# Sums of weights one piece later, and the second pass in the order P3, P7, P6, in a TensorE-bound decoder trunk

## The chip, the core and the metric

The kernel runs on one core of a Trainium2 chip. The metric is the device time of one execution in microseconds; the times before are three runs of the same program, and one further execution was profiled.

## What is computed

Two residual layers on 256 tokens of width 2048: the first has differential attention as its mixer, the second a Mamba-2 mixer, and each mixer is followed by a dense MLP of width 8192. The change lies in the MLPs:

```python
def sq_relu_mlp(h, w1, w2):
    return jnp.square(jax.nn.relu(h @ w1)) @ w2

for i in range(DEPTH):
    hn = rms_norm(h, mixer_norm[i])
    ...
    h = h + mix.astype(h.dtype)
    h = h + sq_relu_mlp(rms_norm(h, mlp_norm[i]), mlp_w1[i], mlp_w2[i]).astype(h.dtype)
```

All inputs are float32. The kernel keeps that accuracy by splitting every operand into a rounded high part and a low rest and by multiplying high by high, high by low and low by high.

## The kernel before

**Weights.** A unit of weights is 128 x 1024 floats (512 KB). `load` (L181) takes one of five `raw` buffers and issues the transfer on SP's queue (L186). `split_weights` (L153) takes one of four `w` buffers: ScalarE casts the raw weights into the high half (L158), and VectorE subtracts that from the raw weights to give the low half (L159). TensorE needs the cast for the first four matmuls of a product and the subtraction for the last two.

**The first matrix of an MLP** is cut into eight column blocks. One is done plainly (`blocks`, kind "s"), seven by a scheme of Strassen's kind (`seven`, L547, kind "S"): a 2 x 2 division of the product with seven products P1 to P7 in place of eight. `product` (L552) issues six 512-column matmuls (L557, L559) for one piece of one product: four with the high half of the weights, two with the low half. The activations' sums (S1 to S4) are made once for an MLP by `sum_parts` (tile `sa`); P1, P2 and P4 use plain activations (tile `act`). The weights' sums are made by VectorE for every unit: L569 (b11 - b12, kept in tile `wsum`), L579 (b22 - b12, in place of b12), L584 (adds b22 to `wsum`), L600 (subtracts b21 from `wsum`). Each of the four lines runs 4 times in a block, 7 blocks in each of two MLPs, 56 times in all.

`seven` is a generator in three passes of four steps. A step of the first pass issues a piece of P1 and one of P5; of the second, P7, P3 and P6; of the third, P2 and P4. Behind every piece it pauses (`yield`).

**What comes in the pauses.** `mlp` (L610) drives the blocks of the next quarter against the second matrix of this one: for each piece of W2 (`token_steps`, L224: a load, a cast, a split and 12 matmuls at L238 and L240) it lets the generator go on by some 58/30 = 1.9 pieces (L699 to L709). In the pauses there are also bits of side work (`side.tick`): the expansion of finished blocks into activations (L640: transposes at L656, cast L263, subtraction L264) and, at the end of a W2 block, the update of the residual (L716). In the first block of an MLP the partner is the plainly done column block (`wide_steps`, L169 and L173).

**PSUM.** P1, P5, P7, P6, P2 and P4 and the transposes share three `aux` slots; P3 has the slot `aux1` alone in the MLP. A slot comes free when VectorE or ScalarE has read it (L264, L574, L575, L587 to L591, L603, L604).

**Order.** The queue of each engine is ordered by the framework in which the kernel is written. It takes the order of the text as a preference and may put forward an instruction whose inputs are ready earlier; on the chip each queue then runs in that fixed order, and the waits between the engines are put in by the framework too.

Of the kernel before, what the change touches and what calls it, by code (L numbers as in the profile page):

```python
# [16 lines left out]
ALU = mybir.AluOpType  # L17
# [74 lines left out]
def trunk_kernel(ctx: ExitStack, tc: tile.TileContext, x, xt, par, rope, qk, wv, wo, w10, w10s, w20, win, wdt, wout, w11, w11s, w21, out):  # L92
    nc = tc.nc
    V, S, G, PE = nc.vector, nc.scalar, nc.gpsimd, nc.tensor
# [23 lines left out]
    def aux():  # L118
        return ps.tile([P, 512], F32, tag="aux", bufs=3, name="aux")

    def aux1():
        return ps.tile([P, 512], F32, tag="aux1", bufs=1, name="aux1")
# [30 lines left out]
    def split_weights(raw, n=1):  # L153
        w = wp.tile([P, 2, 1024], F32R, tag="w", bufs=4, name="w")
        wh, wl = w[:, 0, :], w[:, 1, :]
        for i in range(n):
            s = slice(1024 // n * i, 1024 // n * (i + 1))
            S.copy(out=wh[:, s], in_=raw[:, s])  # L158
            V.tensor_tensor(out=wl[:, s], in0=raw[:, s], in1=wh[:, s].bitcast(F32), op=ALU.subtract)  # L159
        return wh, wl  # L160
# [20 lines left out]
    def load(src, n=1):  # L181

        raw = wp.tile([P, 1024], F32, tag="raw", bufs=5, name="raw")
        w = 1024 // n
        for i in range(n):
            nc.sync.dma_start(out=raw[:, i * w:(i + 1) * w], in_=src[:, i * w:(i + 1) * w])  # L186
        return raw
# [137 lines left out]
    with tc.tile_pool(name="xin", bufs=1) as xp:  # L325
# [13 lines left out]
        for g in range(4):  # L339
# [4 lines left out]
            for b in range(4):  # L344
                c = slice(512 * (g % 2), 512 * (g % 2 + 1))
                src = raw[g // 2][b][:, c]
# [200 lines left out]
    def seven(pool, src, sas, u):  # L547


        a = [None] * 4  # L550

        def product(pp, which, w, i):  # L552
            for j, wj in enumerate(w):
                for kp in range(2):
                    ah, al = sas[2 * i + kp][which]
                    m = wj[:, kp * NB:(kp + 1) * NB]
                    PE.matmul(pp, lhsT=ah, rhs=m, start=(i + kp + j == 0), stop=(i == 3 and kp + j == 2))  # L557
                    if j == 0:
                        PE.matmul(pp, lhsT=al, rhs=m, start=False, stop=False)  # L559

        A11, S4, A12, S1, S3, S2, A22 = range(7)
        p1, p5 = aux(), aux()
        for i in range(4):
            while len(sas) < 2 * i + 2:
                side.tick()
            b11, b12 = load(src[0, i]), load(src[1, i])
            a[i] = pool.tile([P, 1024], F32, tag="wsum", bufs=4, name="wsum")
            w = split_weights(b11)
            V.tensor_tensor(out=a[i], in0=b11, in1=b12, op=ALU.subtract)  # L569
            product(p1, A11, w, i)  # L570
            yield
            product(p5, S1, split_weights(a[i]), i)
            yield
        S.copy(out=u[:, 0, 0], in_=p1)  # L574
        S.copy(out=u[:, 1, 1], in_=p5)  # L575
        p7, p3, p6 = aux(), aux1(), aux()
        for i in range(4):
            b12, b22 = load(src[1, i]), load(src[2, i])
            V.tensor_tensor(out=b12, in0=b22, in1=b12, op=ALU.subtract)  # L579
            product(p7, S3, split_weights(b12), i)  # L580
            yield
            product(p3, S4, split_weights(b22), i)
            yield
            V.tensor_tensor(out=a[i], in0=b22, in1=a[i], op=ALU.add)  # L584
            product(p6, S2, split_weights(a[i]), i)
            yield
        V.tensor_tensor(out=u[:, 0, 1], in0=p6, in1=u[:, 0, 0], op=ALU.add)  # L587
        V.tensor_tensor(out=u[:, 1, 0], in0=p7, in1=u[:, 0, 1], op=ALU.add)
        V.tensor_tensor(out=u[:, 0, 1], in0=u[:, 0, 1], in1=u[:, 1, 1], op=ALU.subtract)
        V.tensor_tensor(out=u[:, 0, 1], in0=p3, in1=u[:, 0, 1], op=ALU.add)  # L590
        V.tensor_tensor(out=u[:, 1, 1], in0=u[:, 1, 0], in1=u[:, 1, 1], op=ALU.subtract)  # L591
        for t in range(2):
            S.activation(u[:, t, 1], u[:, t, 1], AF.Relu)
            S.activation(u[:, t, 1], u[:, t, 1], AF.Square)
        p2, p4 = aux(), aux()
        for i in range(4):
            b21 = load(src[3, i])
            product(p2, A12, split_weights(b21), i)
            yield
            V.tensor_tensor(out=a[i], in0=a[i], in1=b21, op=ALU.subtract)  # L600
            product(p4, A22, split_weights(a[i]), i)
            yield
        V.tensor_tensor(out=u[:, 0, 0], in0=p2, in1=u[:, 0, 0], op=ALU.add)  # L603
        V.tensor_tensor(out=u[:, 1, 0], in0=u[:, 1, 0], in1=p4, op=ALU.subtract)  # L604
        for t in range(2):
            S.activation(u[:, t, 0], u[:, t, 0], AF.Relu)
            S.activation(u[:, t, 0], u[:, t, 0], AF.Square)
        yield

    def mlp(xs, w1, w1s, w2, pool, after):  # L610
# [21 lines left out]
        def hidden(c):  # L632
            us[c] = u = pool.tile([P, 2, 2, NB], F32, tag="u", bufs=2, name="u")
            n = kinds[:c].count(kinds[c])
            if kinds[c] == "s":
                yield from blocks(n, u)
            else:
                yield from seven(pool, w1s[n], sas, u)
# [438 lines left out]
```

## Time and profile before

| what | value |
|---|---|
| median of 3 runs | 2449.77 us (2448.08 to 2452.68) |
| the profiled execution | 2449.62 us, span of its instructions 2447.9 us |
| TensorE matmuls, busy | 2434.1 us, 12050 instructions |
| VectorE, busy | 2098.2 us, 2591 instructions |
| ScalarE, busy | 1535.6 us, 2154 instructions |
| moved by DMA | 500.54 MB, mean 204 GB/s |
| a weight load, issue to landing | 4.3 to 4.4 us in the median for the MLPs' weights |

In the rows PE is TensorE's matmul side and PEld its weight loads, DVE is VectorE, ACT ScalarE, SP the queue that issues the loads. A row of a group gives the line, the engine, the operation, the tile written and those read, the shapes, the count, the busy time with the mean of one in ns, and the idle time just before with what ended it. The span of a matmul is modelled and overlaps the next one, so starts are to be compared rather than ends. The MLPs lie at about 395 to 1070 us and 1740 us to the end; the blocks done by seven products end at about 978 and 2336 us.

### The profile page before, as it was taken

How to read it: one execution, taken by the hardware profiler on the slowest of the kernel's cores; microseconds unless marked ns; L12 is line 12 of the kernel's file. 1: busy time of each engine (PE TensorE's matmuls, PEld its weight loads, DVE VectorE, ACT ScalarE, POOL GpSimd, SP SyncE). 2: the span in 40 equal slices, each digit the busy share in tenths (PEclk: the TensorE clock that was granted, in tenths of full speed). 3: DMA queues.
4: the chain of work that ended last, by engine and by line, in shares of the span. 5: the costliest groups of instructions: out<-in, count | busy, mean ns of one | idle time of the engine just before them, and what ended most of it. 6: DMA issues, size and time to landing. Idle time of an engine off the chain costs nothing.

```text
span 2447.9 us, 32626 instructions
## 1 busy us (share of the span) xinstructions
PE 2434.1 (99%) x12050; PEld 2038.8 (83%) x12050; DVE 2098.2 (86%) x2591; ACT 1535.6 (63%) x2154; POOL 1.2 (0%) x8
## 2 busy tenths in 40 slices
PE   9999999999999999999999999999999999999999
PEld 8888888878888788888888888888887888878887
DVE  6988879999998999568886887887899999899964
ACT  7666656666666666456776575775666666666653
POOL 0000000000000000000000000000000000000000
PEclk9999999999999999999999999999999999999999
DMA  8545555667667676556565556556566766776764
GB/s 287 164 157 175 167 175 194 208 232 243 230 208 230 221 231 218 191 177 211 190 198 196 174 198 199 166 189 191 190 218 220 239 229 203 238 232 206 233 205 147
DMA packets 140192, 500.54 MB, mean 204 GB/s; under 512 B 15648, under 2 KB 15840, under 8 KB 140032
## 3 DMA queue, kind: packets, MB, share of 16 engines
q1 hardware_dynamic: 137312, 489.75, 61.3%
q10 hardware_dynamic: 2720, 8.71, 1.0%
q8 instruction: 94, 1.54, 0.2%
q14 instruction: 66, 0.54, 0.1%
HBM read 496.24 MB, written 2.16 MB: 204 GB/s over the span
## 4 chain that ended last, share of the span: by engine, by line
PE 70%; DVE 18%; DMA 7%; issue 4%; ACT 1%; DVEq 0%; SPq 0%; ACTq 0%
PE pp L238 21%; PE pp L169 16%; DVE w L159 11%; PE pp L240 10%; PE pp L173 9%; PE aux L557 6%; DMA raw<-in_w11s 3%; DMA raw<-in_w10s 3%; PE aux L559 3%; DVE wsum L569 1%; DVE wsum L600 1%; DVE raw L579 1%; PE aux L878 1%; DVE h L716 1%; ACT w L158 1%
## 5 line engine op out<-in xcount | busy, mean ns | idle before, releaser
L159 DVE TENSOR_TENSOR w<-raw,w 128x1024 fp32r<-128x1024 f32 x858 | 1034.6, 1219 | 196.1 <-ACT w L158 193.5
L158 ACT CAST w<-raw 128x1024 fp32r<-128x1024 f32 x858 | 892.7, 1052 | 493.4 <-PE pp L238 316.3
L238 PE MATMUL pp<-w,act 128*128 128x512 f32 x3072 | 983.1, 391 | 0.7 <-ACT w L158 0.7
L238 PEld LDWEIGHTS pp<-w,act 128*128 128x128 f32 x3072 | 575.4, 188 | 121.7 <-ACT w L158 1.5
L240 PE MATMUL pp<-w,act 128*128 128x512 f32 x1536 | 598.5, 390 | 0.0
L169 PE MATMUL pp<-act,w 128*128 128x512 f32 x2000 | 489.0, 392 | 0.0
L169 PEld LDWEIGHTS pp<-act,w 128*128 128x128 f32 x2000 | 366.4, 188 | 72.6 <-issue 1.0
L240 PEld LDWEIGHTS pp<-w,act 128*128 128x128 f32 x1536 | 288.3, 188 | 58.0
L557 PE MATMUL aux<-w,sa 128*128 128x512 f32 x896 | 300.3, 392 | 5.2 <-DVE act L264 1.7
L173 PEld LDWEIGHTS pp<-act,w 128*128 128x128 f32 x2000 | 258.3, 191 | 11.0 <-issue 0.9
L173 PE MATMUL pp<-act,w 128*128 128x256 f32 x2000 | 266.8, 284 | 0.0
L158 ACT CAST w<-wsum 128x1024 fp32r<-128x1024 f32 x168 | 176.9, 1053 | 114.6 <-PE pp L238 43.8
L557 PE MATMUL aux<-w,act 128*128 128x512 f32 x672 | 228.8, 394 | 0.8 <-ACT w L158 0.3
L159 DVE TENSOR_TENSOR w<-wsum,w 128x1024 fp32r<-128x1024 f32 x168 | 204.8, 1219 | 1.9 <-ACT w L158 1.5
L557 PEld LDWEIGHTS aux<-w,sa 128*128 128x128 f32 x896 | 167.4, 188 | 44.3 <-DVE w L159 4.7
L559 PE MATMUL aux<-w,sa 128*128 128x512 f32 x448 | 175.2, 391 | 0.0
L557 PEld LDWEIGHTS aux<-w,act 128*128 128x128 f32 x672 | 124.8, 188 | 32.2 <-DVE w L159 6.2
L559 PE MATMUL aux<-w,act 128*128 128x512 f32 x336 | 131.4, 391 | 0.0
L559 PEld LDWEIGHTS aux<-w,sa 128*128 128x128 f32 x448 | 84.2, 188 | 16.7
L569 DVE TENSOR_TENSOR wsum<-raw 128x1024 f32<-128x1024 f32 x56 | 68.4, 1222 | 21.4 <-DMA raw<-in_w10s 11.5
L579 DVE TENSOR_TENSOR raw<-raw 128x1024 f32<-128x1024 f32 x56 | 68.5, 1222 | 20.4 <-DMA raw<-in_w11s 11.4
L600 DVE TENSOR_TENSOR wsum<-wsum,raw 128x1024 f32<-128x1024 f32 x56 | 68.0, 1220 | 7.4 <-DMA raw<-in_w11s 3.9
(218 smaller groups left out, 1736.0 us busy)
## 6 DMA issues: line engine op xcount, KB each, us to landing
raw<-in_w SPq DMA_DIRECT2D x288, 512.0 KB, 4.4
raw<-in_win SPq DMA_DIRECT2D x160, 512.0 KB, 4.1
raw<-in_w10s SPq DMA_DIRECT2D x140, 512.0 KB, 4.3
raw<-in_w11s SPq DMA_DIRECT2D x140, 512.0 KB, 4.3
raw<-in_wout SPq DMA_DIRECT2D x64, 512.0 KB, 4.1
raw<-in_qk SPq DMA_DIRECT2D x56, 512.0 KB, 4.3
raw<-in_wv SPq DMA_DIRECT2D x32, 512.0 KB, 4.2
raw<-in_wo SPq DMA_DIRECT2D x32, 512.0 KB, 4.2
```

What stands on the lines that cost most here:

```text
L158: S.copy(out=wh[:, s], in_=raw[:, s])
L159: V.tensor_tensor(out=wl[:, s], in0=raw[:, s], in1=wh[:, s].bitcast(F32), op=ALU.subtract)
L169: PE.matmul(acc, lhsT=wk, rhs=acts[k0 + k], start=(start and k == 0), stop=False)
L173: PE.matmul(acc[:, 0, :], lhsT=wk, rhs=acts[k0 + k][:, 0, :], start=False, stop=(stop and k == 7))
L238: PE.matmul(pp[t], lhsT=act[:, 0, tok], rhs=m, start=(s + i + k == 0), stop=(s == n - 1 and i + k == 2))
L240: PE.matmul(pp[t], lhsT=act[:, 1, tok], rhs=m, start=False, stop=False)
L557: PE.matmul(pp, lhsT=ah, rhs=m, start=(i + kp + j == 0), stop=(i == 3 and kp + j == 2))
L559: PE.matmul(pp, lhsT=al, rhs=m, start=False, stop=False)
L569: V.tensor_tensor(out=a[i], in0=b11, in1=b12, op=ALU.subtract)
L579: V.tensor_tensor(out=b12, in0=b22, in1=b12, op=ALU.subtract)
L600: V.tensor_tensor(out=a[i], in0=a[i], in1=b21, op=ALU.subtract)
L716: V.scalar_tensor_tensor(out=h[:, t, cols(j)], in0=pp[t], scalar=r2[:, t:t + 1], in1=h[:, t, cols(j)], op0=ALU.mult, op1=ALU.add)
```

## The change

In the first pass the sum L569 is issued after P1's piece and its pause, right ahead of P5's split. In the second pass b22 is loaded ahead of b12, P3 (which needs b22 alone) becomes the first product of a step, L579 and L584 follow its pause together, then come P7 and P6. The products, the operands and the instructions are the same.

```diff
             b11, b12 = load(src[0, i]), load(src[1, i])
             a[i] = pool.tile([P, 1024], F32, tag="wsum", bufs=4, name="wsum")
             w = split_weights(b11)
+            product(p1, A11, w, i)
+            yield
             V.tensor_tensor(out=a[i], in0=b11, in1=b12, op=ALU.subtract)
-            product(p1, A11, w, i)
-            yield
             product(p5, S1, split_weights(a[i]), i)
             yield
         S.copy(out=u[:, 0, 0], in_=p1)
         S.copy(out=u[:, 1, 1], in_=p5)
         p7, p3, p6 = aux(), aux1(), aux()
         for i in range(4):
-            b12, b22 = load(src[1, i]), load(src[2, i])
+            b22, b12 = load(src[2, i]), load(src[1, i])
+            product(p3, S4, split_weights(b22), i)
+            yield
             V.tensor_tensor(out=b12, in0=b22, in1=b12, op=ALU.subtract)
+            V.tensor_tensor(out=a[i], in0=b22, in1=a[i], op=ALU.add)
             product(p7, S3, split_weights(b12), i)
             yield
-            product(p3, S4, split_weights(b22), i)
-            yield
-            V.tensor_tensor(out=a[i], in0=b22, in1=a[i], op=ALU.add)
             product(p6, S2, split_weights(a[i]), i)
             yield
```

## Rows read from the trace of the kernel before

**Rows 1.** The page: span, busy time by engine, granted clock in 40 slices.

```profile
span 2447.9 us, 32626 instructions
PE 2434.1 (99%) x12050; PEld 2038.8 (83%) x12050; DVE 2098.2 (86%) x2591; ACT 1535.6 (63%) x2154; POOL 1.2 (0%) x8
PEclk9999999999999999999999999999999999999999
```

**Rows 2.** Windows: stretch, length, busy PE, PEld, DVE, ACT, POOL, clock, DMA, GB/s.

```profile
500.00:600.00 100.00, 100.00 (x445) 82.46 (x444) 97.20 (x93) 63.17 (x69) 0.00 (x0) 1.00 0.70 237
...
1900.00:2000.00 100.00, 100.00 (x441) 82.29 (x440) 95.05 (x92) 64.38 (x69) 0.00 (x0) 1.00 0.69 224
```

**Rows 3.** Groups by line: products' weight loads, two sums; idle before and its releasers.

```profile
L557 PEld LDWEIGHTS aux<-w,sa 128*128 128x128 f32 x896 | 167.4, 188 | 44.3 <-DVE w L159 4.7 <-DVE act L264 3.6 <-ACT w L158 2.4
L557 PEld LDWEIGHTS aux<-w,act 128*128 128x128 f32 x672 | 124.8, 188 | 32.2 <-DVE w L159 6.2 <-ACT w L158 1.2 <-issue 0.4
...
L579 DVE TENSOR_TENSOR raw<-raw 128x1024 f32<-128x1024 f32 x56 | 68.5, 1222 | 20.4 <-DMA raw<-in_w11s 11.4 <-DMA raw<-in_w10s 8.7
L569 DVE TENSOR_TENSOR wsum<-raw 128x1024 f32<-128x1024 f32 x56 | 68.4, 1222 | 21.4 <-DMA raw<-in_w10s 11.5 <-DMA raw<-in_w11s 9.9
```

**Rows 4.** Who waited for whom: us in total, times, longest.

```profile
ACT w L158 <- DVE raw L579: 66.9, 37, 3.2
...
ACT w L158 <- DMA raw<-in_w: 5.8, 12, 0.9
```

**Rows 5.** Timeline of VectorE, a second-pass step: start, us, instruction, merged count.

```profile
510.07 1.22 DVE L159 TENSOR_TENSOR w<-raw,w 128x1024 fp32r<-128x1024 f32 x1
511.21 1.22 DVE L579 TENSOR_TENSOR raw<-raw 128x1024 f32<-128x1024 f32 x1
512.34 1.22 DVE L584 TENSOR_TENSOR wsum<-raw,wsum 128x1024 f32<-128x1024 f32 x1
513.60 3.50 DVE L159 TENSOR_TENSOR w<-raw,w 128x1024 fp32r<-128x1024 f32 x3
```

**Rows 6.** Timeline of TensorE, matmuls of a W2 piece.

```profile
511.80 0.39 PE L238 MATMUL pp<-w,act 128*128 128x512 f32 x1
512.03 0.39 PE L240 MATMUL pp<-w,act 128*128 128x512 f32 x1
```

**Rows 7.** Timeline at P6's piece in the second MLP's first block, by engine.

```profile
1800.53 1.23 DVE L579 TENSOR_TENSOR raw<-raw 128x1024 f32<-128x1024 f32 x1 [1.41 <-DMA raw<-in_w11s]
...
1798.43 1.04 ACT L158 CAST w<-wsum 128x1024 fp32r<-128x1024 f32 x1
...
1801.11 0.39 PE L559 MATMUL aux<-w,sa 128*128 128x512 f32 x1
1802.94 0.73 PE L557 MATMUL aux<-w,sa 128*128 128x512 f32 x2 [1.45 <-DVE w L159]
```

**Rows 8.** Timeline at the start of a later block, VectorE and TensorE.

```profile
826.72 1.23 DVE L569 TENSOR_TENSOR wsum<-raw 128x1024 f32<-128x1024 f32 x1 [1.31 <-DMA raw<-in_w10s]
...
830.32 1.28 DVE L264 TENSOR_TENSOR act<-aux,act 128x512 fp32r<-128x512 f32 x2
...
831.05 0.50 PE L557 MATMUL aux<-w,sa 128*128 128x512 f32 x1 [1.19 <-DVE act L264]
```

**Rows 9.** Timeline where P5 follows its sum at once, VectorE, ScalarE, TensorE.

```profile
487.78 1.22 DVE L569 TENSOR_TENSOR wsum<-raw 128x1024 f32<-128x1024 f32 x1
...
489.09 1.05 ACT L158 CAST w<-wsum 128x1024 fp32r<-128x1024 f32 x1 [0.43 <-DVE wsum L569]
...
490.19 0.51 PE L557 MATMUL aux<-w,sa 128*128 128x512 f32 x1 [0.76 <-DVE u L604]
...
501.67 1.22 DVE L569 TENSOR_TENSOR wsum<-raw 128x1024 f32<-128x1024 f32 x1
...
1861.27 1.05 ACT L158 CAST w<-wsum 128x1024 fp32r<-128x1024 f32 x1 [0.63 <-DVE wsum L569]
```

More of the change, by code (lines that the diff above doesn't have):

```diff
@@ L568, in seven @@
             w = split_weights(b11)
-            V.tensor_tensor(out=a[i], in0=b11, in1=b12, op=ALU.subtract)
             product(p1, A11, w, i)
             yield
+            V.tensor_tensor(out=a[i], in0=b11, in1=b12, op=ALU.subtract)
             product(p5, S1, split_weights(a[i]), i)
```

## The prediction, made before the changed kernel was run

> **What bounds the kernel now.** I read the page first, then the windows over the MLP stages, then the groups by line, the waits, and last the timeline around the few places where TensorE stands. The page says that PE is busy in 2434.1 of 2447.9 us, at the full granted clock in every slice [rows 1]. The windows show the stages that the change touches: PE is busy in all of 500 to 600 and of 1900 to 2000, and VectorE in over 95% of each [rows 2]. VectorE's rows overlap a little: they last 1.22 us and start 1.13 to 1.14 us apart [rows 5], so its real load is some 7% lower. A busy PE need not be a fast one, so I looked at its pace: 512-column matmuls start 0.23 us apart [rows 6], one behind the other. TensorE is the bound, and what the change can win is the time in which TensorE waits for the weights of the seven products.
>
> That time is small. The weight loads of the products with sums on the activation side (P5, P7, P3, P6) sat idle for 44.3 us, but the part with a named releaser is 4.7 us for a split's second half on VectorE, 3.6 us for the L264 that frees a PSUM slot, and 2.4 us for a cast on ScalarE: 10.7 us together [rows 3]. The products on plain activations (P1, P2, P4) add 6.2 and 1.2 us [rows 3]; nothing in the change reaches P2 and P4, and P1's split only loses a neighbour.
>
> **The change part by part.** Nothing is removed or added: 224 sums (56 on each of four lines, of which 168 change their place), 280 loads and 392 splits stay. The profiled execution took 2449.62 us, 1.7 more than its span [rows 1] and 0.15 less than the median of the three runs, 2449.77; the sum is made against 2449.62.
>
> *The text's order is not the queue's order.* In the text of before, the sum of L584 stands behind both splits of its pass-2 step and behind two pauses in which other work is issued. On VectorE it ran directly behind L579, at 512.34, and three splits came after it [rows 5]. So the framework puts first what is ready, and the text only decides between things that are ready together. The moved sums therefore move less than their lines do.
>
> *Second pass, P3 ahead of P7, b22 loaded first (56 steps: 12 matmuls and two loads on SP's queue change places in each).* Before, the first product of a step, P7, needs both loads, L579 (1.22 us) and a cast (1.05 us); ScalarE waited 66.9 us for L579 in all [rows 4]. After, the first product needs one load and one cast, and P7 comes six matmuls later, 6 x 0.23 = 1.4 us more slack. L579 needs both loads in either order, so the swap on SP's queue neither delays nor hastens it. What is it worth on PE? Bound from below: all of the 4.7 us for splits [rows 3]; from above: nothing, since P7's slack only grows and P3's chain gets shorter by the sum. No PE wait that I followed ends at P7's or P3's cast in steady state, so I take 0 here.
>
> *P6's split behind a blocked L579.* This is the one place where the sums cost PE visibly. At 1800.53 L579 starts after 1.41 us of idle VectorE, held by the landing of b22; behind it stands the split of P6's weights, whose cast had begun at 1798.43 and taken 1.05 us, so it could have run before 1800. P6's last two matmuls name that split as what they waited for: they start at 1802.94 where 1801.11 + 0.23 = 1801.34 was their turn, 1.6 us lost [rows 7]. With b22's own split now ahead of L579 in the text, VectorE has other work at that moment and the older P6 split wins when both are ready. Bounds: 0 (L579 is still put first, as its inputs land at the same time) and 4.7 us (all of the idle on splits [rows 3]). I take the single place that I can see whole, 1.6 us.
>
> *First pass, L569 behind P1's matmuls and the pause.* On VectorE nothing of P1 stands; what it is moved past is what the pause issues: a load, a cast and a split of a W2 piece, sometimes L264 of the expansion or L716. Those waiting for L569 are the cast of P5's weights and then P5. Bound from above: the places where P5 follows its sum at once. At the start of the third block the sum at 487.78 ends at 489.00, the cast starts at 489.09, P5 at 490.19 [rows 9]; there are four such places, two at 487.78 and 501.67 and two in the second MLP, the last with its cast at 1861.27 [rows 9]. One W2 split (1.14 us [rows 5]) and one L264 (two in a row take 1.28 us, so some 0.6 each [rows 8]) ahead of each sum would cost 4 x 1.74 = 7.0 us. Bound from below: L569 itself holds things up. At 826.72 it starts after 1.31 us of waiting for a load, and the L264 that frees P5's PSUM slot comes only at 830.32, so P5 waits until 831.05 [rows 8]; 3.6 us of such waits in all [rows 3]. In the other 52 places the cast or the product comes later than that. Between -3.6 and +7.0 I take 0, because the queue goes by readiness [rows 5] and L569 is ready at the same moment as before.
>
> *Third line moved, L584.* It already runs where the new text puts it [rows 5]: 0.
>
> *Buffers.* b12 of the first pass may hold its one of five raw buffers for a VectorE operation longer, which would put off the next load on SP by 1.14 us. ScalarE's waits on loads of W2 come to 5.8 us in 12 times [rows 4]. Bounds 0 and +5.8 us; I take 0, since loads are mostly early and a cast's wait is not PE's.
>
> Sum: 2449.62 - 1.6 = 2448.0 us, 0.07% below. About 0.2%, 4.9 us, is what a measurement of this kernel can tell from no change, so my forecast is no change.
>
> **The rivals.** *Faster: what stands behind the sums goes.* If the scheduler really keeps L569 and L579 behind older splits and behind L264, both the 4.7 us of splits and the 3.6 us of PSUM slots [rows 3] go: 2449.62 - 8.3 = 2441.3 us. For it: VectorE idles 21.4 us ahead of L569 and 20.1 us ahead of L579 waiting for loads (11.5 + 9.9, 11.4 + 8.7) [rows 3], and everything queued behind waits too. Against it: that needs nearly every such place cured, and list order by readiness tends to put the sum back where it was.
>
> *Slower: P5 becomes the late one.* The place is the first pass at the start of a block, where P5 has no slack [rows 9]. If the W2 split and an L264 go ahead of the sum, the price is the 7.0 us above: 2456.6 us. It decides as soon as VectorE has something else ready when b12 lands; one split alone would be 4 x 1.14 = 4.6 us, still inside what cannot be told from none. For it: VectorE is over 95% busy there [rows 2]. Against it: the sum needs no weight buffer and is mostly ready early.
>
> *The change does little in the queues.* L584 shows that a line's place can be without effect [rows 5]. If the queues come out nearly the same, the time is 2449.6 us, inside my forecast's case.
>
> *VectorE is the bound.* Then its 41.5 us of idle before the sums [rows 3] would be real time: 2408.1 us. Against it is TensorE's own pace of 0.23 us without gaps [rows 6]. The Trainium skill's page "TensorE: Matmul & The Clock Gate", section "Back-to-back issue gap", gives about 131 ns per 512-column matmul as the sustained roofline; by it TensorE could run far ahead and VectorE would set the pace, with 2408.1 us as the sum. The trace disagrees: its matmuls start 0.23 us apart where nothing waits, closer to the 216 ns that the page gives for an isolated one.
>
> **How the numbers follow.** My forecast has 0.40 and the case of little effect 0.15; both lie within 0.2%, so same is 0.55. Faster: 0.24 for the first rival and 0.01 for the last, 0.25. Slower: 0.20. The likeliest is 2448.0 us. The range reaches down to the first rival's 2441.3 and up to the second's 2456.6, with half a microsecond on either side for their own sizes: 2441.0 to 2457.0. That is no wider than the bounds: all of the 10.7 us would give 2438.9, and the costs of P5 and of the buffers together 2462.4.
>
> **What would show it.** Right: 12050 matmuls, 0.23 us apart, and the stages of 500 to 600 and 1900 to 2000 as full as now; at the second MLP's first block no 1.4 us of idle VectorE between P6's cast and P6's split; the weight loads of the products on sums idle less than 4.7 us for a split; ScalarE's wait for L579 far below 66.9 us. Each step can fail by itself: P6's step, if L579 still stands ahead of that split; the first pass, if P5's idle for a cast grows past 2.4 us; the buffers, if PE or ScalarE name loads more often. The prediction as a whole is wrong if PE's idle time in the MLP stages changes by more than 5 us, or if a wait appears in a stage that the diff does not touch, since a new order of the queues may carry on into what follows.

## The result, and the profile after

The changed kernel took 2461.76 us in the median of four runs (2458.17 to 2465.51), the kernel before 2449.45 us beside it (four runs, 2448.08 to 2452.68). The ratio is 1.0045, with a 95% interval of 1.0033 to 1.0057: some 11 us slower. The forecast was no change, 2448.0 us, and the range ended at 2457.0. The profiled execution of the changed kernel took 2458.17 us.

The page of the changed kernel, its span, busy times and granted clock, against [rows 1]:

```profile
span 2456.4 us, 32582 instructions
PE 2437.6 (99%) x12050; PEld 2037.2 (83%) x12050; DVE 2099.5 (85%) x2591; ACT 1537.4 (63%) x2154; POOL 1.2 (0%) x8
PEclk9999999999999999999999999999999999999999
```

The matmuls, their clock and the work of VectorE and ScalarE are as before; the span is 8.5 us longer. So the time went into waiting, and the windows say that it did so in the stages that the diff touches: PE, busy in all of both stretches in [rows 2], now stands for 0.82 us of the first and 0.18 us of the second.

```profile
500.00:600.00 100.00, 99.18 (x440) 81.20 (x439) 95.87 (x90) 64.05 (x70) 0.00 (x0) 1.00 0.73 240
1900.00:2000.00 100.00, 99.82 (x437) 81.15 (x436) 92.90 (x91) 62.41 (x67) 0.00 (x0) 1.00 0.71 225
```

The groups by line of the changed kernel. L571 is the first pass's sum (L569 before), L581 P7's sum (L579), L582 P6's sum (L584); L600 kept its number. Against [rows 3], to which the last two rows here, of the kernel before, are added:

```profile
L557 PEld LDWEIGHTS aux<-w,sa 128*128 128x128 f32 x896 | 166.6, 188 | 50.8 <-DVE w L159 11.0 <-ACT w L158 4.1 <-DVE act L264 2.9
...
L582 DVE TENSOR_TENSOR wsum<-raw,wsum 128x1024 f32<-128x1024 f32 x56 | 68.5, 1223 | 17.4 <-DMA raw<-in_w11s 9.7 <-DMA raw<-in_w10s 7.6
L571 DVE TENSOR_TENSOR wsum<-raw 128x1024 f32<-128x1024 f32 x56 | 68.5, 1223 | 24.4 <-DMA raw<-in_w10s 13.7 <-DMA raw<-in_w11s 10.7
L581 DVE TENSOR_TENSOR raw<-raw 128x1024 f32<-128x1024 f32 x56 | 68.4, 1221 | 4.4 <-DMA raw<-in_w11s 2.5 <-DMA raw<-in_w10s 1.8
L600 DVE TENSOR_TENSOR wsum<-wsum,raw 128x1024 f32<-128x1024 f32 x56 | 67.9, 1222 | 15.3 <-DMA raw<-in_w11s 7.8 <-DMA raw<-in_w10s 7.4
...
L584 DVE TENSOR_TENSOR wsum<-raw,wsum 128x1024 f32<-128x1024 f32 x56 | 68.2, 1218 | 0.0
L600 DVE TENSOR_TENSOR wsum<-wsum,raw 128x1024 f32<-128x1024 f32 x56 | 68.0, 1220 | 7.4 <-DMA raw<-in_w11s 3.9 <-DMA raw<-in_w10s 3.5
```

Two things are to be seen. The weight loads of the products on sums idle for a split's low half 11.0 us instead of 4.7, and for casts 4.1 instead of 2.4. And VectorE's waiting for loads has changed its place: 20.4 us stood before L579, now 4.4 stand before the same sum, but 17.4 before P6's sum, and 15.3 before L600. P6's sum (L584 before) had waited for no load at all, and L600 for 7.4 us.

The waits of the changed kernel, against [rows 4]:

```profile
ACT w L158 <- DVE raw L581: 25.9, 19, 3.0
PEld aux L557 <- DVE w L159: 17.7, 38, 1.6
ACT w L158 <- DMA raw<-in_w: 16.0, 11, 2.0
```

ScalarE waits for P7's sum 25.9 us where it waited 66.9. That is what the change does for P7, and it bought nothing. Its waits for loads of W2 (in_w) went from 5.8 to 16.0 us, and TensorE's waits for a split from 10.9 us in 27 cases (the 4.7 and 6.2 us of [rows 3]) to 17.7 in 38.

**The third block of each MLP.** The first stretch where TensorE falls behind lies at the place of [rows 9]. VectorE, ScalarE and TensorE of the changed kernel there (start, us, instruction, count, idle before):

```profile
488.47 0.68 DVE L264 TENSOR_TENSOR act<-u,act 128x512 fp32r<-128x512 f32 x1
489.07 0.68 DVE L603 TENSOR_TENSOR u<-aux,u 128x512 f32<-128x512 f32 x1
489.68 1.22 DVE L571 TENSOR_TENSOR wsum<-raw 128x1024 f32<-128x1024 f32 x1
...
489.79 0.64 ACT L606 ACTIVATE u<-u 128x512 f32<-128x512 f32 x1 [0.38 <-DVE u L603]
490.46 0.63 ACT L607 ACTIVATE u<-u 128x512 f32<-128x512 f32 x1
491.00 1.03 ACT L158 CAST w<-wsum 128x1024 fp32r<-128x1024 f32 x1
...
492.08 0.50 PE L557 MATMUL aux<-w,sa 128*128 128x512 f32 x1 [1.45 <-ACT w L158]
```

Before, the sum started at 487.78, directly behind a split, and its cast at 489.09 [rows 9]. Now an L264 and L603, which reads a product of the block before (P2), stand ahead of it on VectorE, and the two activations that L603 releases stand ahead of the cast on ScalarE. P5 starts after 1.45 us for a cast, where it had waited 0.76 us for L604. At 1853.62 the second MLP shows the same, with 1.43 us.

**A blocked sum ahead of a split.** VectorE, then TensorE, near the end of the first MLP's blocks in the changed kernel:

```profile
949.91 1.22 DVE L159 TENSOR_TENSOR w<-wsum,w 128x1024 fp32r<-128x1024 f32 x1
952.47 1.23 DVE L600 TENSOR_TENSOR wsum<-wsum,raw 128x1024 f32<-128x1024 f32 x1 [1.33 <-DMA raw<-in_w10s]
953.61 3.49 DVE L159 TENSOR_TENSOR w<-raw,w 128x1024 fp32r<-128x1024 f32 x3
...
954.88 0.98 PE L557 MATMUL aux<-w,sa 128*128 128x512 f32 x3 [1.15 <-DVE w L159]
```

L600 holds VectorE for 1.33 us because its load has not landed, and three splits stand behind it, started one behind the other as soon as it is through. TensorE reaches the low half of P3 and waits 1.15 us. (The Trainium skill's page "PSUM — Partial Sum Buffer", section "Engine vs sequencer instructions", calls VectorE's queue a strict first-in-first-out; the trace agrees, since none of the three splits passes the 1.33 us.) The same picture stands at 535.61 (0.82 us, behind an L581 that waited 1.02) and at 2315.96 (0.97 us, behind an L600 that waited 1.17).

### The profile page after: what moved, and what is told of

The parts are those of the page before. It is cut to its first block, busy times and chain, and to the rows that moved or that the text cites. A ratio compares the mean times of both kernels' runs of the same rounds, so it can differ in the third digit from the quotient of the medians.

```text
span 2456.4 us, 32582 instructions
## 1 busy us (share of the span) xinstructions
PE 2437.6 (99%) x12050; PEld 2037.2 (83%) x12050; DVE 2099.5 (85%) x2591; ACT 1537.4 (63%) x2154; POOL 1.2 (0%) x8
## 4 chain that ended last, share of the span: by engine, by line
PE 68%; DVE 18%; DMA 9%; issue 4%; ACT 1%; DVEq 0%; SPq 0%; ACTq 0%
PE pp L238 20%; PE pp L169 16%; DVE w L159 11%; PE pp L240 10%; PE pp L173 9%; PE aux L557 6%; DMA raw<-in_w10s 5%; DMA raw<-in_w11s 4%; PE aux L559 3%; DVE wsum L582 1%; DVE wsum L571 1%; DVE raw L581 1%; PE aux L878 1%; ACT w L158 1%; DVE wsum L600 1%
## 5 line engine op out<-in xcount | busy, mean ns | idle before, releaser
L571 DVE TENSOR_TENSOR wsum<-raw 128x1024 f32<-128x1024 f32 x56 | 68.5, 1223 | 24.4 <-DMA raw<-in_w10s 13.7
L582 DVE TENSOR_TENSOR wsum<-raw,wsum 128x1024 f32<-128x1024 f32 x56 | 68.5, 1223 | 17.4 <-DMA raw<-in_w11s 9.7
L600 DVE TENSOR_TENSOR wsum<-wsum,raw 128x1024 f32<-128x1024 f32 x56 | 67.9, 1222 | 15.3 <-DMA raw<-in_w11s 7.8
```

## The experiments

Each kernel ran on one chip beside runs of the kernel before. Where a ratio is turned into microseconds, it is multiplied with 2449.

**The two passes apart.** First the first pass's edit alone, then the second pass's edits alone.

```diff
 e1_pass1 (against before)
             w = split_weights(b11)
-            V.tensor_tensor(out=a[i], in0=b11, in1=b12, op=ALU.subtract)
             product(p1, A11, w, i)
             yield
+            V.tensor_tensor(out=a[i], in0=b11, in1=b12, op=ALU.subtract)
 e2_pass2 (against after)
             w = split_weights(b11)
+            V.tensor_tensor(out=a[i], in0=b11, in1=b12, op=ALU.subtract)
             product(p1, A11, w, i)
             yield
-            V.tensor_tensor(out=a[i], in0=b11, in1=b12, op=ALU.subtract)
```

> Only the first pass has the new order; the second pass is as before. Theory A (the second pass costs it: the sum L582 for P6 needs b22 alone, which now lands first, so it is put far ahead on VectorE and holds up the splits of P7 behind a load) expects 2449.5 to 2451.5 us, the excess being the later start of P5 at the start of the third column block, 0.7 us in each MLP. Theory C (the cost is P5 coming late in the first pass) expects most of the 12.3 us here: 2458 us or more.

> Only the second pass has the new order; the first pass is as before. Theory A expects 2459 to 2462 us and weight loads of the products on sums that idle for 10 us or more on splits (11.0 in the changed kernel, 4.7 before). Theory C expects about 2450 us.

Measured: the first pass alone 2454.77 us, 1.0024 [1.0015, 1.0032], 5.9 us; the second alone 2455.48 us, 1.0025 [1.0014, 1.0036], 6.1 us. Both lose, and together they make up the 1.0045 within the intervals. Neither theory is met: each expected nearly the whole loss in one pass. When the n-th matmul of this first kernel is laid beside the n-th of the kernel before, TensorE falls back 3.8 us between 487 and 555 us and 3.2 us between 1848 and 1916, and keeps its distance nearly everywhere else (9.1 us behind at the end of this execution). That is the start of the third block of each MLP. It begins with P5, which waits longer for its cast than the 0.76 us of [rows 9]; the rest comes in the work that follows:

```profile
491.95 0.50 PE L557 MATMUL aux<-w,sa 128*128 128x512 f32 x1 [1.97 <-ACT w L158]
...
1854.26 0.50 PE L557 MATMUL aux<-w,sa 128*128 128x512 f32 x1 [1.96 <-ACT w L158]
```

**The third block left as it was.** The first-pass edit in every block but the third:

```diff
-            w = split_weights(b11)
-            V.tensor_tensor(out=a[i], in0=b11, in1=b12, op=ALU.subtract)
+            w = split_weights(b11); late or V.tensor_tensor(out=a[i], in0=b11, in1=b12, op=ALU.subtract)
             product(p1, A11, w, i)
             yield
+            if late: V.tensor_tensor(out=a[i], in0=b11, in1=b12, op=ALU.subtract)
...
-                yield from seven(pool, w1s[n], sas, u)
+                yield from seven(pool, w1s[n], sas, u, c != 2)
```

> The kernel before, with the new order of the first pass in every column block but the third, at whose start P5 follows its sum at once. Theory S (the first pass costs only at that start, where the sum now stands behind an L264 and L603 on VectorE): 2448 to 2451 us, like the kernel before. Rival (every first-pass sum comes a little late): most of the 5.5 us of the first pass alone, so 2453 us or more.

Measured: 2448.39 us, 1.0003 [0.9994, 1.0012]. The loss is gone, so the cost of the first pass sits in the third block, and the later sum in the other twelve blocks costs nothing that can be measured.

**The parts of the second pass.** First the changed kernel with the old order of the loads; then the kernel before with the new order of the loads alone; then with the new order of the products alone.

```diff
 e3_oldloads (against after)
-            b22, b12 = load(src[2, i]), load(src[1, i])
+            b12, b22 = load(src[1, i]), load(src[2, i])
 e7_swap_alone (against before)
-            b12, b22 = load(src[1, i]), load(src[2, i])
+            b22, b12 = load(src[2, i]), load(src[1, i])
 e8_order_alone (against before)
+            product(p3, S4, split_weights(b22), i)
+            yield
             V.tensor_tensor(out=b12, in0=b22, in1=b12, op=ALU.subtract)
+            V.tensor_tensor(out=a[i], in0=b22, in1=a[i], op=ALU.add)
             product(p7, S3, split_weights(b12), i)
             yield
-            product(p3, S4, split_weights(b22), i)
-            yield
-            V.tensor_tensor(out=a[i], in0=b22, in1=a[i], op=ALU.add)
```

> The changed kernel, but b12 is loaded ahead of b22 as before. Theory A: the sum for P6 and the sum for P7 are ready at the same moment again, so the former is not put ahead: 2449 to 2453 us, and the P6 sum's own idle time on loads falls from 17.4 us to under 5. Theory B (P7 comes later in a step, so its raw buffer is held longer and all later loads are late): no change from the changed kernel, 2459 to 2463 us, with ScalarE's waits on loads of W2 near 16 us.

> The kernel before with one edit: in the second pass b22 is loaded ahead of b12; the order of sums and products stays. Theory A (b22 first makes P6's sum L584 ready first, so it is put far ahead on VectorE and blocks there on loads) expects 2452 to 2457 us, and L584's own idle time on loads over 10 us instead of 0. Theory B (what costs is P7 coming later in a step) expects 2448 to 2451 us.

> The kernel before with the second pass in the order P3, P7, P6 and the sums behind P3, but the loads and the first pass as before. Theory A: 2449 to 2452 us. Theory B: 2454 to 2457 us.

Measured: old loads 2456.03 us, 1.0031 [1.0019, 1.0043]; the loads alone 2461.20 us, 1.0052 [1.0039, 1.0064]; the products alone 2451.54 us, 1.0010 [1.0001, 1.0019]. With the old loads the idle before P6's sum falls from 17.4 to 0.0 us, as theory A had it, but the time stays above its range. The largest single cost is an exchange of two loads that I had taken as neutral: 12.7 us in the old product order, more than the whole change and above the range of either theory. Putting P3 first softens it, since both second-pass edits together lose 6.1 us. The groups of the kernel with the loads alone:

```profile
L557 PEld LDWEIGHTS aux<-w,sa 128*128 128x128 f32 x896 | 166.3, 188 | 56.2 <-DVE w L159 16.5 <-ACT w L158 5.0 <-DVE act L264 2.1
...
L584 DVE TENSOR_TENSOR wsum<-raw,wsum 128x1024 f32<-128x1024 f32 x56 | 68.4, 1221 | 20.9 <-DMA raw<-in_w10s 11.1 <-DMA raw<-in_w11s 9.4
...
L579 DVE TENSOR_TENSOR raw<-raw 128x1024 f32<-128x1024 f32 x56 | 68.3, 1219 | 3.9 <-DMA raw<-in_w11s 2.5 <-DMA raw<-in_w10s 1.3
L600 DVE TENSOR_TENSOR wsum<-wsum,raw 128x1024 f32<-128x1024 f32 x56 | 67.9, 1219 | 14.8 <-DMA raw<-in_w11s 8.5 <-DMA raw<-in_w10s 6.1
```

L584 needs b22 alone (and `wsum`, made a pass earlier). With b22 loaded first it is the first thing that becomes ready, and the framework queues it far ahead on VectorE: before its step's P7 sum in 44 of 56 steps (48 in the changed kernel), where the kernel before has it behind that sum in all 56. On the chip it stands there until b22 lands, 20.9 us in all, with splits behind it. In the changed kernel P6's matmuls start 12.8 us in the median behind the end of their sum, against 7.6 us before: the sum is early and nobody wants it yet.

**P6's sum held behind P7's.** If the place in the queue is the cause, the loads may stay exchanged. The first kernel is the changed one with that order, the second the kernel before with the loads exchanged and that order:

```diff
 e4_sum_order (against after)
-            V.tensor_tensor(out=b12, in0=b22, in1=b12, op=ALU.subtract)
-            V.tensor_tensor(out=a[i], in0=b22, in1=a[i], op=ALU.add)
+            d = V.tensor_tensor(out=b12, in0=b22, in1=b12, op=ALU.subtract)
+            with tc.issue_after(d.ins):
+                V.tensor_tensor(out=a[i], in0=b22, in1=a[i], op=ALU.add)
 e12_swap_held (against the loads alone)
-            V.tensor_tensor(out=b12, in0=b22, in1=b12, op=ALU.subtract)
+            d = V.tensor_tensor(out=b12, in0=b22, in1=b12, op=ALU.subtract)
...
-            V.tensor_tensor(out=a[i], in0=b22, in1=a[i], op=ALU.add)
+            with tc.issue_after(d.ins): V.tensor_tensor(out=a[i], in0=b22, in1=a[i], op=ALU.add)
```

> The changed kernel, but on VectorE's queue the sum for P6 is held behind the sum for P7 of the same step; loads and products keep the new order. Theory A: 2448 to 2453 us; the idle time on loads moves from the P6 sum (17.4 us) to the P7 sum (4.4 us). Theory B: 2459 to 2463 us, since the buffers are held as long as in the changed kernel.

> The kernel before with b22 loaded ahead of b12, and P6's sum (L584) held on VectorE behind P7's sum (L579). Compared row by row, the queues of all engines are those of the kernel before; only the two loads of a second-pass step stand the other way round on SP. Theory A (the swap costs through the order it gives to VectorE, since P6's sum is ready with b22 alone and is put far ahead): 2447 to 2452 us, idle before L584 back to about 0 us (20.9 with the swap alone). Rival B (the swap costs by itself: b12 lands one load later, so P7's sum and split are late): 2456 to 2462 us, and the idle before L579 on loads well above the 20.4 us of before.

Measured: the changed kernel with it 2458.37 us, 1.0033 [1.0021, 1.0046]; the loads alone with it 2449.42 us, 1.0001 [0.9992, 1.001]. The second settles it: the two loads are still exchanged and the time is that of before. Its groups:

```profile
L557 PEld LDWEIGHTS aux<-w,sa 128*128 128x128 f32 x896 | 167.4, 188 | 42.4 <-DVE act L264 3.4 <-DVE w L159 3.0 <-ACT w L158 2.1
...
L579 DVE TENSOR_TENSOR raw<-raw 128x1024 f32<-128x1024 f32 x56 | 68.4, 1222 | 20.5 <-DMA raw<-in_w11s 11.4 <-DMA raw<-in_w10s 8.7 <-DVE w L159 0.4
...
L584 DVE TENSOR_TENSOR wsum<-raw,wsum 128x1024 f32<-128x1024 f32 x56 | 68.2, 1219 | 0.0
```

20.5 us before L579 and 0.0 before L584 are the values of before: only which sum is blocked, and what stands behind it, made the 12.7 us. The first kernel stayed above what the theory gave it, since that left out the third block's cost; 1.0033 is close to the first pass and the product order together (1.0024 and 1.0010).

**The opposite direction.** Three tries to better the kernel before: P7's sum (L579) queued behind the split of P6 before it; the first-pass sum ahead of b11's split; both.

```diff
 e9_p6_first (against before)
-            V.tensor_tensor(out=wl[:, s], in0=raw[:, s], in1=wh[:, s].bitcast(F32), op=ALU.subtract)
+            last_sub[0] = V.tensor_tensor(out=wl[:, s], in0=raw[:, s], in1=wh[:, s].bitcast(F32), op=ALU.subtract).ins
...
-            product(p5, S1, split_weights(a[i]), i)
+            w = split_weights(a[i]); p6_sub = last_sub[0]; product(p5, S1, w, i)
...
-            V.tensor_tensor(out=b12, in0=b22, in1=b12, op=ALU.subtract)
+            with tc.issue_after(p6_sub): V.tensor_tensor(out=b12, in0=b22, in1=b12, op=ALU.subtract)
...
-            product(p6, S2, split_weights(a[i]), i)
+            w = split_weights(a[i]); p6_sub = last_sub[0]; product(p6, S2, w, i)
 e11_sum_first (against before)
-            w = split_weights(b11)
             V.tensor_tensor(out=a[i], in0=b11, in1=b12, op=ALU.subtract)
+            w = split_weights(b11)
 e10_sums_placed: both
```

> The kernel before with one order added: P7's sum (L579) is queued on VectorE behind the split of P6 (at the first step: of P5) that precedes it in the text. Theory A (the 1.6 us at 1802 was P6's split behind a blocked sum, and a late P7 sum costs nothing): 2446.5 to 2449 us. Rival B (a sum put later makes P7 late, as in the first pass of the third block, and splits lose their place): 2451 to 2457 us, and idle of the weight loads on sums named for L159 above 8 us (4.7 before).

> The kernel before with the first-pass sum (L569) issued ahead of the split of b11 instead of behind it, the opposite direction to the change. Theory A (P5's chain at the start of the third block is the only place where this sum decides; earlier is better there): 2446 to 2449 us, with the waits of P5 at about 492 and 1853 us shorter than the 0.92 us of before. Rival B (the blocked sum now stands ahead of P1's split as well): 2451 to 2456 us, with idle of P1's weight loads for L159 above 10 us (6.2 before).

> A try for a faster kernel than before: the first pass's sum is written ahead of the split of b11, and the second pass's P7 sum L579 is held behind the split of the preceding P6 (P5 in the first step) on VectorE's queue. If the waits at P6's split (some 2.5 us in all) and at the start of the third block (up to 1.1 us in each MLP) go and no others come, 2444 to 2447 us. If the order at VectorE only moves the waits to other splits, 2449 us or more.

Measured: P7's sum held 2460.1 us, 1.005 [1.0037, 1.0063]; the sum first 2449.07 us, 1.0001 [0.9992, 1.001]; both 2455.33 us, 1.0029 [1.0017, 1.004]. None is better. Holding P7's sum takes L579's waits for loads from 20.4 to 5.8 us, and makes ScalarE wait for it 132.4 us instead of 66.9; TensorE's weight loads of the products on sums then idle 10.0 us for casts, against 2.4. The sum first does shorten the wait at the third block (P5's 0.76 us of [rows 9] is gone, 0.41 us for a split is left), but not the time.

**What is left when both costs are undone.** The changed kernel with P6's sum held and the third block's first pass in the old order; then with the third block's sum ahead of b11's split; then with the old first pass in the other blocks as well.

```diff
 e13_both_undone: the edits of e4_sum_order and of e6_not_block2, on after
 e14_sum_ahead (against e13_both_undone)
-            w = split_weights(b11); late or V.tensor_tensor(out=a[i], in0=b11, in1=b12, op=ALU.subtract)
+            if not late: V.tensor_tensor(out=a[i], in0=b11, in1=b12, op=ALU.subtract)
+            w = split_weights(b11)
 e15_sum_ahead_old (against e14_sum_ahead)
             w = split_weights(b11)
+            if late == 2: V.tensor_tensor(out=a[i], in0=b11, in1=b12, op=ALU.subtract)
             product(p1, A11, w, i)
             yield
-            if late: V.tensor_tensor(out=a[i], in0=b11, in1=b12, op=ALU.subtract)
+            if late == 1: V.tensor_tensor(out=a[i], in0=b11, in1=b12, op=ALU.subtract)
...
-                yield from seven(pool, w1s[n], sas, u, c != 2)
+                yield from seven(pool, w1s[n], sas, u, 0 if c == 2 else 2)
```

> The changed kernel with both suspected costs undone and everything else kept: P6's sum held on VectorE behind P7's sum, and the first pass in the old order in the third block alone. Theory A (these two and the product order are the whole loss, and they add up): only the cost of the product order is left, ratio about 1.001, 2450 to 2453 us, and the idle before P6's sum about 0 us. Rival B (the loads swapped or the sums moved in the other blocks cost by themselves, or the parts act on each other): 2455 to 2460 us. Rival C (without its two faults the change helps): below 2447 us.

> The kernel with both costs undone, and in the third block the first-pass sum issued ahead of the split of b11. There the product order had left the sum on VectorE behind L603 of the block before, so that two activations stood ahead of its cast on ScalarE (P5 waited 1.47 us at 490.7 and at 1850.2); in this kernel the sum is queued ahead of L603. Theory A (what is left of the loss, 1.0018, sits mostly at this place): 2448.5 to 2451 us, and P5's wait there below 0.8 us. Rival B (it is spread over the other blocks): 2452 to 2455 us, though P5's wait there goes.

> The same, with the first pass of before in all blocks but the third (the sum ahead of P1's piece, behind the split): the second pass alone is changed, with P6's sum held behind P7's. Theory A: 2448 to 2451 us, no better than the one above, since the sums of the other blocks were found to cost nothing in the old product order. Rival B (in the new product order the later sums of the other blocks cost too): 2 us or more below the one above.

Measured: 2453.91 us, 1.0018 [1.0009, 1.0027]; 2453.61 us, 1.0024 [1.0015, 1.0033]; 2452.9 us, 1.0024 [1.0014, 1.0033]. Undoing the two takes the loss from 4.5 to 1.8 per mille, less far than theory A gave it, and the rest is not P5's wait at the third block. Putting the sum ahead there removes that wait whole (no wait of TensorE between 486 and 496 us in the second kernel) and the time does not move. When the n-th matmul starts (us) in the kernel before and in the first two of these kernels, one execution each:

```
matmul   before   e13_both_undone   e14_sum_ahead
2550     499.0    498.6             497.2
2800     555.2    555.5             556.0
9450     1859.7   1860.3            1858.4
9700     1916.4   1918.4            1917.6
```

The 1.4 us that the second kernel has won over the first at 499 are given back by 555, and of the 1.9 us won in the second MLP 0.8 are left at 1916. What ScalarE and TensorE meet on the way, in the second kernel:

```profile
517.05 1.05 ACT L158 CAST w<-raw 128x1024 fp32r<-128x1024 f32 x1 [1.78 <-DMA raw<-in_w]
...
533.58 1.05 ACT L158 CAST w<-raw 128x1024 fp32r<-128x1024 f32 x1 [1.92 <-DMA raw<-in_w]
...
550.98 1.23 ACT L595 ACTIVATE u<-u 128x512 f32<-128x512 f32 x2 [3.49 <-DVE u L592]
...
553.16 1.03 ACT L158 CAST w<-wsum 128x1024 fp32r<-128x1024 f32 x1
...
554.24 0.50 PE L557 MATMUL aux<-w,act 128*128 128x512 f32 x1 [1.05 <-ACT w L158]
```

Loads of W2 come late, but the wait of TensorE at 554.24 does not end with one of them: its cast at 553.16 is of a sum and stands behind four activations, the first of which waited for VectorE's L592. What loses the 1.4 us is thus not shown. For the late loads, the waits of the product order alone, then of the kernel before and of the changed one, name who holds back the load queue (SPq is the queue that issues the loads):

```profile
SPq L186 <- DVE wsum L582: 39.8, 20, 3.2
...
ACT w L158 <- DMA raw<-in_w: 14.9, 13, 2.1
...
SPq L186 <- DVE wsum L584: 3.9, 2, 1.9
...
SPq L186 <- DVE raw L581: 11.3, 6, 1.9
...
SPq L186 <- DVE wsum L582: 3.6, 4, 1.1
```

With the product order alone, b22's raw buffer is held until P6's sum has read it, and 20 loads wait for that, 39.8 us of the load queue's time; in the kernel before two did (3.9 us). Six of the thirteen late loads of W2 there follow directly on such a load. In the changed kernel, where P6's sum comes early, four do (3.6 us), and six wait for P7's sum, which also reads b22 (11.3 us); yet ScalarE's waits for W2 are as long there, and ten of the eleven loads that it waited for were issued when a split had let go of a buffer. So b22's buffer is named for the product order alone and not for the changed kernel. ScalarE's waits for W2 lie between 14.9 and 26.7 us in all eight kernels with the new product order and between 1.2 and 5.8 us in all eight with the old one, before among them. How many microseconds of the product order's loss are this wait was not isolated: a sixth raw buffer might show it and was not tried.

## Why the prediction was wrong, step by step

**What bounds the kernel.** Right: TensorE, at its own pace, and the change decides only over its waits for weights. Two steps failed behind that: the exchange of the loads, which the prediction put at nothing, and the first pass, which it put at 0 and which is the larger of the two in the changed kernel.

**Second pass: "the swap on SP's queue neither delays nor hastens it".** This step failed by its mechanism. The sentence is true of L579 and was asked of the wrong sum. I did not ask which instruction becomes ready first when b22 comes first: P6's sum, which needs b22 alone. It went to the head of VectorE's queue and stood there for its load. Alone the swap costs 12.7 us and with the same queue as before 0.2 us, so the mechanism is shown; beside P3 first it is some 3 us (the changed kernel, 1.0045, against the one with old loads, 1.0031, and the one with the sum held, 1.0033), but these intervals overlap, so that its size there is not clear of noise. I had read the rule that decides it myself, that the framework puts first what is ready [rows 5], and had used it only to show that a line's place is without effect.

**"It already runs where the new text puts it" (L584: 0).** Wrong with the loads exchanged, right without: with the old loads, and with the sum held, its idle time is 0.0 us as before.

**Second pass: P7's slack, 0.** The product order alone costs 2.5 us [0.2 to 4.7], with the bound set from 0 downwards. ScalarE's wait for P7's sum fell as the step said, from 66.9 to 25.9 us, and was worth nothing, since those waits had been covered.

**P6's split, -1.6 us.** The place was read rightly. The sum of that step waits for its second load in all four traces that have the second pass and the loads of before: 1.41 us [rows 7], and in the kernels with the first pass alone, with the third block left as it was and with the sum first:

```profile
1805.10 1.23 DVE L579 TENSOR_TENSOR raw<-raw 128x1024 f32<-128x1024 f32 x1 [1.29 <-DMA raw<-in_w11s]
...
1797.95 1.23 DVE L579 TENSOR_TENSOR raw<-raw 128x1024 f32<-128x1024 f32 x1 [1.22 <-DMA raw<-in_w11s]
...
1801.70 1.23 DVE L579 TENSOR_TENSOR raw<-raw 128x1024 f32<-128x1024 f32 x1 [0.92 <-DMA raw<-in_w11s]
```

TensorE then waits for P6's split 1.45, 1.35, 0.17 and 0.97 us. The wait at 1802.94 is not there in the changed kernel, as forecast. Neither is it in the kernel with exchanged loads and the queues of before, whose ratio is still 1.0001: 1.6 us are too few to be seen in the time of the whole. In the changed kernel other splits more than took its place, with 11.0 us of idle for splits against 4.7.

**First pass, taken as 0 between -3.6 and +7.0.** It measured +5.9 us, near the upper bound. What failed is the reason for the 0, "the queue goes by readiness [rows 5] and L569 is ready at the same moment as before": at the start of the third block the new place in the text did put the sum behind other work, and P5's wait grew from 0.76 to 1.97 us. The rival that I called slower (P5 becomes the late one, at the start of the third block) named the right place. That its price of 7.0 us is near is luck in part: it was four places at 1.74 us, and the trace shows two, at 3.8 and 3.2 us with what follows them. What I had against it, that the sum is mostly ready early, fits the other blocks, where the move costs nothing that can be measured, and did not help there. The instructions that got ahead are an L264 and L603, with two activations on ScalarE, rather than a split of W2. It was given a chance of 0.20 and its time of 2456.6 us would have been 1.8 us too high for the first pass alone.

**Buffers, taken as 0 between 0 and +5.8.** ScalarE's waits for W2 rose by 10.2 us (5.8 to 16.0), more than the bound. They do not rise with the first pass alone (4.4 us) but with every kernel that has P3 first, so the step looked at the wrong pass. With the product order alone b22's buffer is held longer; what makes the loads late in the changed kernel, and their share of the time, are open.

**The rivals faster, little effect, and VectorE as the bound** all fell. Against the last: with P7's sum held, VectorE idled 36.7 us before its four sums instead of 49.2, and the kernel was 12.2 us slower. The sum by the runs: 5.9 us for the first pass, 2.5 us for the product order and some 3 us for the exchanged loads beside it, 11.4 us, against 11.0 us measured. The third term is itself taken from the changed kernel; an independent sum is that of the first two, 1.0024 and 1.0010, against 1.0031 with both and the old loads. The parts do not simply add everywhere: with both costs undone 1.0010 was due and 1.0018 [1.0009, 1.0027] measured, and that rest is open.

## What to carry to other kernels

Where a framework orders queues by readiness, ask of every exchanged load which instruction it makes ready first, and what will then stand behind that instruction on its engine while the load is on its way; an early sum on an in-order queue costs whatever is queued behind it. Slack is to be looked for at the start of blocks, one by one, since a move that costs nothing measurable in twelve blocks cost 5.9 us in two. Whether a wait for a load belongs to the order or to one execution is told by other traces with the same order; and a wait that is rightly found may still be replaced by others when the order changes.

## What the runs showed that was not expected

Waits for loads of about a microsecond came back from execution to execution at the same instruction: P7's sum in the second step of the second MLP's first block waited 1.41, 1.29, 1.22 and 0.92 us in four kernels. It waited for nothing with the loads exchanged and the same compute queues. And a wait that was removed can come back: the 1.4 us that TensorE had won at 499 us were lost again by 555 us, with the same time for the whole as before the cure.
